# Squares of the group norms on GpSimd, edge copies on ScalarE alone, one modulation group moved from layer 0's gate/up to layer 1's

## The chip, the cores and the metric

The kernel runs on one core of a Trainium2 chip. The metric is the device time of one execution in microseconds (us); three runs of the kernel before gave 2403.01, 2403.49 and 2408.04 us, a median of 2403.49 us. Everything is float32 outside; most matrix products are made from operands split into a high and a low part in the fp32r format.

## The reference

Two layers over 1024 tokens of width 1024. In each layer six vectors (shift, scale and gate for attention and for the feed-forward part) come from a small vector `c`; each of these twelve is called a modulation group here, numbered (layer, group).

```python
for l in range(DEPTH):                                   # DEPTH = 2
    mod = silu(c) @ w_mod[l] + b_mod[l]
    sh_a, sc_a, gt_a, sh_f, sc_f, gt_f = split(mod, 6)   # groups 0..5
    h = rms_norm(x, g_attn[l]) * (1 + sc_a) + sh_a
    # 4 heads A (neighbourhood), 6 heads B (sliding window, sink), 6 heads C (dense)
    ya, yb, yc = attentions(split(h @ w_in[l]))
    y = concat(rms_norm(ya, ga), rms_norm(yb, gb), rms_norm(yc, gc))   # group norms
    x = x + gt_a * (y @ w_o[l])
    h = rms_norm(x, g_ffn[l]) * (1 + sc_f) + sh_f
    gate, up = split(h @ w_gu[l])
    x = x + gt_f * ((silu(gate) * up) @ w_down[l])
return rms_norm(x, g_final)
```

## The kernel before

Each layer runs through the same stages: input projection, attention, output projection, gate/up, down. TensorE (PE) makes all products, VectorE (DVE) and ScalarE (ACT) empty the PSUM banks, split operands and do the softmax, GpSimd (POOL) scales rows and takes some elementwise work, SyncE (SP) issues the DMAs.

**Attention.** One loop over `n` works through 64 pairs of query blocks (24 pairs of C, then 16 of A, then 24 of B; four pairs p = 0 to 3 to a head). A and B heads see a band of keys; their pairs are of class `Band`, and this stretch is called the band. In iteration `n` of the band the engines run in the order in which the code is written (they are pinned): POOL scales the probabilities of pair n+2 (`divide`), DVE makes the low part of pair n-1's turned block (`low`) and adds up the output of pair n-3 (`combine`, tile `y`), PE makes the scores of pair n+4, ACT the exponentials of pair n+3, PE turns pair n's probabilities (`turn`, tiles `T`), and PE multiplies pair n-2 with the values (`pv`). A turned pair has one tile with the four inner blocks and one with the edge blocks (one block of 128x128 for p = 0 and 3, two for p = 1 and 2). ACT casts the inner tile to its high part; the edge tile is copied to the tile `edge`, by DVE for even p and by ACT for odd p. There is one PSUM bank for `pv`, shared by two pairs: after the odd pair, ACT copies half of it (`fold`, tile `cmb`), DVE adds (`combine`), and only then may PE start the next even pair's `pv`.

**Group norms.** When the two heads of a 128-row chunk of `y` are done, `norm_sum` squares the chunk in two halves of 128x512 on ACT, and POOL adds the square to a running sum `gss` (the first chunk of a group is written to `gss` directly). The halves are put into iterations `n + 1` and `n + 2`; the very last chunk's are done on the spot. Some iterations later the sums become factors, and POOL scales the finished chunks with `y<-y,rb`, one 128x512 tile per iteration. ACT also splits finished chunks for the output projection (`y_split`, tile `qk<-y`).

**Modulation groups.** A group needs 1024x1024 weights, times `silu(c)`, summed over rows. DVE does it: 16 steps of 128x512 (`mod_add`, tile `acc`), each after a DMA (`wmt`); then, for each half, DVE splits the sum (`acch`, `accl`), PE sums it over the partitions with two matmuls (`ps_mod`), and DVE picks the diagonal. Groups (0,2) to (0,4) are made during layer 0's attention stage. `mod_stream` spreads further ones over gate/up as a generator:

```python
mods_due = mod_stream(psl, (ntp, "sq", 2, H), (1, 3))   # all groups before (1, 3)
...
    if q >= EARLY:
        next(mods_due, None)
```

So layer 0's gate/up makes (0,5), (1,0), (1,1), (1,2); layer 1's attention stage makes (1,3), (1,4), (1,5); layer 1's gate/up none.

**Gate/up.** 22 column blocks `q` of seven half-size products each (Strassen-like, `PRODUCTS`, index `i`); a product is 12 matmuls of 128x512 into `ps_w`. The first seven `q` take two products each ahead of the loop. DVE and POOL make the sums and low parts of the weights (`ws`, `wpt`), add up products (`u`, `sg`). PE, ACT and DVE are not pinned here; a scheduler has placed their instructions, and each engine runs them in that order. SP's queue is in program order.

All instructions go through one recording helper, so the profile gives nearly all of them line 49; they are told apart by their tiles.

Of the kernel before, what the change touches and what calls it, by code (L numbers as in the profile page):

```python
# [13 lines left out]
AF = mybir.ActivationFunctionType  # L14
ALU = mybir.AluOpType
# [8 lines left out]
H = 512  # L24
# [61 lines left out]
def trunk(ctx: ExitStack, tc, A, C, out):  # L86
    nc = tc.nc
    pe, act, dve, pool, sp = (
        Engine(tc, e) for e in (nc.tensor, nc.scalar, nc.vector, nc.gpsimd, nc.sync)
    )  # L90
# [214 lines left out]
    def mod_add(k, acc, st):  # L305
        ck = condT[:, k : k + 1]
        if k == 0:
            dve.tensor_scalar(out=acc, in0=st, scalar1=ck, scalar2=None, op0=ALU.mult)
        else:
            dve.scalar_tensor_tensor(  # L310
                out=acc, in0=st, scalar=ck, in1=acc, op0=ALU.mult, op1=ALU.add
            )
# [12 lines left out]
    def mod_parts(c, shared):  # L325
        pl, tag, bufs, width = shared
        acc = going["acc"]
        hi = pl.tile([P, width], F32R, name="acch", tag=tag, bufs=bufs)
        lo = pl.tile([P, width], F32R, name="accl", tag=tag, bufs=bufs)
        dve.tensor_copy(hi, acc[:, c])  # L330
        dve.tensor_tensor(out=lo, in0=acc[:, c], in1=f32(hi), op=ALU.subtract)
        going["parts"] = c.start, hi, lo, shared
# [25 lines left out]
    def mod_stream(psp, shared, until):  # L358


        pl, tag, bufs, width = shared
        acc = None
        while todo and todo[0] < until:
            l, g = todo[0]
            first = going["step"]
            if first == 0:
                going["acc"] = cp.tile([P, 1024], F32, name="acc", tag="acc")
            acc = going["acc"]
            halves = [(k, c0) for k in range(first, KC) for c0 in range(0, 1024, width)]
            loads = {}  # L370

            def load(i):
                k, c0 = halves[i]
                st = loads[i] = pl.tile([P, width], F32, name="wmt", tag=tag, bufs=bufs)
                g0 = g * 1024 + c0
                sp.dma_start(st, A["w_mod"][l, k * P : (k + 1) * P, g0 : g0 + width])

            if halves:
                load(0)
                yield  # L380
            for i, (k, c0) in enumerate(halves):
                if i + 1 < len(halves):
                    load(i + 1)
                mod_add(k, acc[:, c0 : c0 + width], loads.pop(i))
                yield
            going["step"] = KC
            mod_parts(slice(0, width), shared)
            while going["step"]:
                yield
                yield  # L390
                mod_flush(psp)
            yield
# [140 lines left out]
    ps_cm, psl = open_pool("ps0", bufs=8, space=PSUM)  # L533
# [285 lines left out]
    for l in range(2):  # L819
# [358 lines left out]
        for oc in range(NE, 8):  # L1178
            w = wab
            for half in range(2):  # L1180
# [3 lines left out]
                if oc == 6 and half == 0:  # L1184
                    close(ps_cm)
                    psS_cm, psS = open_pool("psS", bufs=2, space=PSUM)
                    ps_cm, psl = open_pool("ps2", bufs=4, space=PSUM)
# [8 lines left out]
                i = 2 * (oc - NE) + half  # L1196
# [14 lines left out]
        y = yp.tile([P, 8, S], F32, name="y")  # L1211
# [12 lines left out]
        def gss_tile():  # L1224
            return atp.tile([P, S], F32, name="gss", tag="gss", bufs=1)
# [4 lines left out]
        gss = {23: gss_tile()}  # L1230
        def pt_tile():
            return wp.tile([P, 4, 256], F32R, name="pt", tag="whl", bufs=8)
# [7 lines left out]
        def t_tile():  # L1240
            return psT.tile([P, 4, P], F32, name="T", tag="T")
# [157 lines left out]
        class Band(Pair):  # L1399
# [42 lines left out]
            def turn(self):  # L1442
                pr = self.pr
                T, self.pt = t_tile(), [pt_tile() for _ in range(2)]
                for b in range(2):
                    for i in range(2):
                        pe.transpose(
                            T[:, 2 * b + i, :], pr[:, b, (1 - b + i) * P : (2 - b + i) * P], ident
                        )
                edges = [pr[:, 0, 0:P]] * self.left + [pr[:, 1, 2 * P : 3 * P]] * self.right  # L1450
                E = t_tile()
                for i, src in enumerate(edges):
                    pe.transpose(E[:, i, :], src, ident)
                hi, lo = (
                    t[:, 0:2, :].rearrange("p i (c q) -> p c i q", c=2) for t in self.pt
                )
                T = T.rearrange("p (c i) q -> p c i q", c=2)
                act.copy(hi, T)
                e = self.e = atp.tile([P, 2, P], F32, name="edge", tag="edge", bufs=3)
                (act.copy if self.p % 2 else dve.tensor_copy)(  # L1460
                    e[:, 0 : len(edges)], E[:, 0 : len(edges)]
                )
                self.low = lambda: sub(lo, T, f32(hi))

            def pv(self):
# [38 lines left out]
                return self.z[:, a:b]  # L1504


        def norm_sum(chunks, ss, last, half):

            n = chunks[last]
            c = slice(half * H, (half + 1) * H)  # L1510
            if last == 0:
                act.activation(ss[:, c], y[:, n, c], AF.Square)
                return
            sq = atp.tile([P, H], F32, name="gsq", tag="rb", bufs=2)
            act.activation(sq, y[:, n, c], AF.Square)
            pool.tensor_tensor(out=ss[:, c], in0=ss[:, c], in1=sq, op=ALU.add)

        def norm_scale(chunks, r, psp, tag, engines):
# [76 lines left out]
        N = len(stream)  # L1595
# [5 lines left out]
        for n in range(-AHEAD - 1, N + 3):  # L1601
# [74 lines left out]
            m = n - 1 if n <= NC else n - 3  # L1676
            for end, (chunks, width) in norms.items():
                if begins[end] <= m <= end and (m - begins[end]) % 8 == 7 and (n <= NC or m >= NC):
                    i = (m - begins[end]) // 8
                    if end not in gss:  # L1680
                        gss[end] = gss_tile()
                    for half in range(2):
                        what = lambda a=(chunks, gss[end], i, half): norm_sum(*a)
                        if m == N - 1:
                            what()
                        else:
                            later.setdefault(n + 1 + half, []).append(what)
                    if m == end and end < N - 1:

                        def stats(end=end, width=width, n=n, chunks=chunks):  # L1690
                            r = rstd_cols([gss[end]], width, 8, atp, psT, tag="T", newton=True)

                            def scale():
                                todo = norm_scale(chunks, r, psT, "T", (pool, pool))
                                for i, what in enumerate(todo):
                                    later.setdefault(n + 9 + i, []).append(what)

                            later.setdefault(n + 8, []).append(scale)

                        later.setdefault(n + 5, []).append(stats)  # L1700
# [8 lines left out]
        ps_cm, psl = open_pool("ps1", bufs=4, space=PSUM)  # L1709
# [65 lines left out]
        nt_cm, ntp = open_pool("nt", side="left")  # L1775
# [80 lines left out]
        ps_cm, psl = open_pool("ps3", bufs=8, space=PSUM)  # L1856
# [135 lines left out]
        EARLY = 7  # L1992
# [29 lines left out]
            shifted_sub(b21, b21, shift(2 * i + 1), t2)  # L2022
            h_split("t4", i, b21, dve)

        mods_due = mod_stream(psl, (ntp, "sq", 2, H), (1, 3))
        bs = []
        rows = None
        norm = rstd_rows(ssq, ntp, psl)
# [1 line left out]
        for q in range(EARLY):  # L2030
            for i in range(2):
                a = [w[:, 4 * i : 4 * i + 4] for w in early[q]]
# [20 lines left out]
        for q in range(NF):  # L2053
            if q % 2 == 0:
                gu_start(q // 2)
            if q < EARLY:
                up = q % 2
                e = sg[q // 2][0][:, 0:H]
                if up:
                    (pool if q > 1 else dve).tensor_tensor(  # L2060
                        out=e, in0=e, in1=quads[q]["11"], op=ALU.mult
                    )
            for i, p in enumerate(PRODUCTS[2 if q < EARLY else 0 :]):
                gu_product(q, p, ahead.get())
                if i == 1 and q < EARLY and not up:
                    act.activation(e, quads[q]["11"], AF.Silu)
                ahead.fill()
                g_step()
                if q >= EARLY:
                    next(mods_due, None)  # L2070
        for _ in mods_due:
            pass
# [30 lines left out]
        nt_cm, ntp = open_pool("nt", side="left")  # L2103
# [98 lines left out]
        def square(n, half, tag, bufs):  # L2202
            sq = ntp.tile([P, H], F32, name="sq", tag=tag, bufs=bufs)
            act.activation(sq, xt[:, n, half * H : (half + 1) * H], AF.Square)
            return sq
# [32 lines left out]
        for u in range(NU):  # L2238
            i, t = divmod(u, NB)
# [13 lines left out]
            a, b = ahead.have.pop(0)  # L2253
# [11 lines left out]
            if t < NB - 1:  # L2265
                continue
            m, half = {
                1: (0, 0), 2: (0, 0), 6: (0, 1), 7: (1, 1), 4: (1, 0), 5: (1, 1), 3: (0, 1),
            }[num]
# [132 lines left out]
```

## Time and profile before

| | before |
|---|---|
| runs | 2403.01, 2403.49, 2408.04 us (median 2403.49) |
| profiled execution, its own time | 2405.66 us |
| its span | 2403.9 us, 33342 instructions, mean granted clock 0.993 |
| busy | PE 2337.2, PE weight loads 1954.9, DVE 1756.9, ACT 1192.2, POOL 744.0 us |
| layer 0: C heads, band, gate/up | about 260 to 383, 383 to 491, 590 to 1014 us |
| layer 1: band, gate/up | about 1556 to 1664, 1760 to 2180 us |

A row of the timeline gives start and duration in us, engine, operation, tile written and tiles read, shape, count, and in brackets the idle time of the engine just before it with what ended that. Rows merged with a count give the time of the whole group. In the tables by window, `(x28)` is the number of instructions that ran in that stretch.

### The profile page before, as it was taken

Reading aid. Unit: us, or ns where it says so; the run is one execution under the profiler, and the core shown is the slowest. Engines: PE = TensorE matmul, PEld = TensorE weight load, DVE = VectorE, ACT = ScalarE, POOL = GpSimd, SP = SyncE. Lnnn points to the kernel's source line nnn. Section 1 sums busy time; section 2 is a strip of 40 time slices with the busy share of each in tenths; the row PEclk is TensorE's granted clock in tenths of the full one; section 3 lists DMA queues with packets and bytes.
Section 4 is the critical chain, followed back from the end, with each engine's and each line's share of the span. In section 5 each row is a group of like instructions: output and inputs, shape, how many; then the busy total and the mean of one; then the engine's idle time right before and its main releaser. Section 6 shows DMA issues by size and latency. Waiting matters only on the chain. (4 is left out here: it accounts for less than half of the span.)

```text
span 2403.9 us, 33342 instructions
## 1 busy us (share of the span) xinstructions
PE 2337.2 (97%) x11733; PEld 1954.9 (81%) x11733; DVE 1756.9 (73%) x2788; ACT 1192.2 (50%) x2250; POOL 744.0 (31%) x719
## 2 busy tenths in 40 slices
PE   8999999999999999999999999999999999999998
PEld 4788899888787887888887879988888888888886
DVE  5767898977858788587677679988797554547765
ACT  3422788944543333344543148897454334334443
POOL 1431345610244443300036114465004443430001
PEclk9999999999999999999999999999999999999999
DMA  8458316154345454586424761152534333329633
GB/s 265 138 183 278 94 62 156 45 201 129 109 137 171 155 186 152 174 265 197 155 88 123 246 215 28 44 145 74 199 103 145 114 101 106 122 88 298 213 125 110
DMA packets 305336, 356.95 MB, mean 148 GB/s; under 512 B 51964, under 2 KB 221788, under 8 KB 305168
## 3 DMA queue, kind: packets, MB, share of 16 engines
q1 hardware_dynamic: 283296, 342.07, 44.9%
q10 hardware_dynamic: 21504, 12.59, 2.0%
q8 instruction: 92, 1.51, 0.3%
q14 instruction: 76, 0.62, 0.1%
q0 software_dynamic: 368, 0.17, 0.0%
HBM read 269.79 MB, written 88.63 MB: 149 GB/s over the span
## 5 line engine op out<-in xcount | busy, mean ns | idle before, releaser
L49 PE MATMUL ps_d<-wpt 128*128 128x512 f32 x1848 | 423.8, 390 | 1.1 <-ACT wpt L49 0.7
L49 PEld LDWEIGHTS ps_d<-wpt 128*128 128x128 f32 x1848 | 345.7, 188 | 74.4 <-issue 3.0
L49 POOL TENSOR_SCALAR pr<-pr,rs 128x1024 f32<-128x1024 f32 (+2 forms) x248 | 193.0, 791 | 220.8 <-DVE rs L49 196.8
L49 POOL TENSOR_TENSOR sg<-sg,u 128x512 f32<-128x512 f32 x82 | 116.6, 1422 | 354.0 <-ACT sg L49 228.4
L49 PE MATMUL pv<-pt,vs 128*128 128x256 f32 x1088 | 175.8, 296 | 17.7 <-DVE y L49 13.4
L49 DVE TENSOR_TENSOR pt<-T,pt 128x512 fp32r<-128x512 f32 x272 | 176.9, 678 | 8.3 <-ACT pt L49 8.0
L49 ACT CAST wpt<-w 128x512 fp32r<-128x512 f32 x154 | 95.7, 621 | 174.6 <-PE ps_d L49 156.1
L49 ACT CAST pt<-T 128x512 fp32r<-128x512 f32 x272 | 151.8, 584 | 40.6 <-PE T L49 38.8
L49 ACT COPY u<-ps_w 128x512 f32<-128x512 f32 x128 | 75.1, 587 | 190.1 <-PE ps_w L49 190.1
L49 POOL TENSOR_TENSOR wpt<-ws,wpt 128x512 fp32r<-128x512 f32 x80 | 110.9, 1388 | 186.5 <-ACT wpt L49 140.3
L49 DVE TENSOR_TENSOR wpt<-w,wpt 128x512 fp32r<-128x512 f32 x154 | 108.9, 707 | 79.8 <-ACT wpt L49 77.7
L49 PEld LDWEIGHTS pv<-pt,vs 128*128 128x128 f32 x1088 | 141.7, 190 | 30.8 <-DVE y L49 26.0
L49 PE MATMUL T<-identr,pr 128*128 128x128 f32 x1176 | 161.6, 273 | 0.8 <-DVE edge L49 0.4
L49 PEld LDWEIGHTS T<-identr,pr 128*128 128x128 f32 x1176 | 137.9, 140 | 16.0 <-issue 1.3
L49 DVE SCALAR_TENSOR_TENSOR acc<-wmt,condT,acc 128x512 f32<-128x512 f32 (+1 forms) x98 | 113.9, 1172 | 44.6 <-DMA wmt<-in_w_mod_dram 44.2
L49 ACT CAST wpt<-ws 128x512 fp32r<-128x512 f32 x176 | 107.8, 622 | 60.0 <-issue 28.1
L49 DVE TENSOR_TENSOR wpt<-ws,wpt 128x512 fp32r<-128x512 f32 x96 | 82.9, 872 | 62.0 <-ACT wpt L49 61.9
L49 DVE TENSOR_TENSOR wpt<-graw,wpt 128x512 fp32r<-128x512 f32 x154 | 110.1, 715 | 17.4 <-ACT wpt L49 17.4
L49 ACT CAST wpt<-graw 128x512 fp32r<-128x512 f32 x154 | 95.0, 617 | 52.9 <-DMA graw<-gpd 48.8
L49 DVE TENSOR_REDUCE rs<-sC 128x1 f32<-128x1024 f32 x88 | 107.3, 1221 | 17.7 <-PE sC L49 12.3
L49 DVE TENSOR_TENSOR ws<-wr 128x512 f32<-128x512 f32 x88 | 78.9, 899 | 53.9 <-POOL wpt L49 50.8
L49 PE MATMUL sC<-qk 128*128 128x512 f32 x384 | 107.5, 403 | 5.8 <-ACT pr L49 5.6
(300 smaller groups left out, 5938.0 us busy)
## 6 DMA issues: line engine op xcount, KB each, us to landing
wr<-in_w_gu_dram SPq DMA_DIRECT2D x92, 512.0 KB, 4.1
gpd<-sg SPq DMA_DIRECT2D x154, 256.0 KB, 4.4
graw<-gpd SPq DMA_DIRECT2D x76, 512.0 KB, 3.5
w<-in_w_down_dram SPq DMA_DIRECT2D x110, 256.0 KB, 5.6
wmt<-in_w_mod_dram SPq DMA_DIRECT2D x48, 512.0 KB, 5.3
qk<-qkd SPq DMA_DIRECT2D x44, 512.0 KB, 7.1
wst<-in_w_o_dram SPq DMA_DIRECT2D x32, 512.0 KB, 4.1
wmt<-in_w_mod_dram SPq DMA_DIRECT2D x64, 256.0 KB, 3.6
```

Of the source, the lines that this page charges most:

```text
L49: ins = op(*args, **kwargs)
```

## The change

Three edits. In `Band.turn`, all edge copies go to ACT; those of even p (20 pairs a layer) were on DVE. In `norm_sum`, the square of a chunk is made by POOL as a product of the chunk with itself, except for the last chunk of the layer; that is 14 of 16 squares a layer. In gate/up, layer 0's stream ends before (1,2) and layer 1's stream makes what is left; since the attention stage of layer 1 still makes three groups, these are now (1,2), (1,3), (1,4), and (1,5) falls into layer 1's gate/up. The stream is asked for a step only after five of the seven products of a `q` (not for i = 2 and 5).

```diff
-                (act.copy if self.p % 2 else dve.tensor_copy)(
-                    e[:, 0 : len(edges)], E[:, 0 : len(edges)]
-                )
+                act.copy(e[:, 0 : len(edges)], E[:, 0 : len(edges)])
...
-        def norm_sum(chunks, ss, last, half):
+        def norm_sum(chunks, ss, last, half, late):
...
+            def square(out):
+                if late:
+                    act.activation(out, y[:, n, c], AF.Square)
+                else:
+                    pool.tensor_tensor(out=out, in0=y[:, n, c], in1=y[:, n, c], op=ALU.mult)
+
             if last == 0:
-                act.activation(ss[:, c], y[:, n, c], AF.Square)
+                square(ss[:, c])
                 return
             sq = atp.tile([P, H], F32, name="gsq", tag="rb", bufs=2)
-            act.activation(sq, y[:, n, c], AF.Square)
+            square(sq)
             pool.tensor_tensor(out=ss[:, c], in0=ss[:, c], in1=sq, op=ALU.add)
...
-                        what = lambda a=(chunks, gss[end], i, half): norm_sum(*a)
+                        what = lambda a=(chunks, gss[end], i, half, m == N - 1): norm_sum(*a)
...
-        mods_due = mod_stream(psl, (ntp, "sq", 2, H), (1, 3))
+        mods_due = mod_stream(psl, (ntp, "sq", 2, H), (1 + l, 2 - 2 * l))
...
-                if q >= EARLY:
+                if q >= EARLY and i % 3 != 2:
                     next(mods_due, None)
```

ACT in layer 0's band, among the B heads: `pr` with 385 columns is an exponential, `pt<-T` the cast of the inner blocks, `edge` the copy of the edge blocks, `gsq` a square, `cmb` the copy that frees the `pv` bank. Before, from one `cmb` to the next:

```order
L49 ACTIVATE pr,rs<-pr,rs 128x385 x2
L49 CAST pt<-T 128x2x2x128
L49 ACTIVATE pr,rs<-pr,rs 128x385 x2
L49 CAST pt<-T 128x2x2x128
L49 COPY edge<-T 128x128
L49 ACTIVATE gsq<-y 128x512
L49 COPY cmb<-pv 64x512
```

The same place now:

```order
L49 ACTIVATE pr,rs<-pr,rs 128x385 x2
L49 CAST pt<-T 128x2x2x128
L49 COPY edge<-T 128x256
L49 ACTIVATE pr,rs<-pr,rs 128x385 x2
L49 CAST pt<-T 128x2x2x128
L49 COPY edge<-T 128x128
L49 COPY cmb<-pv 64x512
```

The square is gone from the place just ahead of `cmb`, and the edge copy of the even pair stands between the two pairs of exponentials.

POOL in layer 0's band, at the change from A to B heads, where it also scales the finished C chunks (`y<-y,rb`); `pr<-pr,rs` is the scaling of probabilities. Before:

```order
L49 TENSOR_SCALAR pr<-pr,rs 128x384 x2
L49 COPY pr<-sinkc 128x2
L49 TENSOR_TENSOR y<-y,rb 128x512
L49 TENSOR_SCALAR pr<-pr,rs 128x384 x2
L49 COPY pr<-sinkc 128x2
L49 TENSOR_TENSOR y<-y,rb 128x512
L49 TENSOR_SCALAR pr<-pr,rs 128x384
L49 TENSOR_SCALAR pr<-pr,rs 128x256
```

The same place now:

```order
L49 TENSOR_SCALAR pr<-pr,rs 128x384 x2
L49 COPY pr<-sinkc 128x2
L49 TENSOR_TENSOR y<-y,rb 128x512
L49 TENSOR_TENSOR gss<-y 128x512
L49 TENSOR_SCALAR pr<-pr,rs 128x384 x2
L49 COPY pr<-sinkc 128x2
L49 TENSOR_TENSOR y<-y,rb 128x512
L49 TENSOR_TENSOR gss<-y 128x512
L49 TENSOR_SCALAR pr<-pr,rs 128x384
L49 TENSOR_SCALAR pr<-pr,rs 128x256
```

Two squares stand in two iterations that also hold a scaling of `y`; the scalings of probabilities behind them come later in POOL's row.

DVE in layer 1's gate/up, at the end of a column block `q`. Before:

```order
L49 TENSOR_TENSOR ws<-wr 128x512
L49 TENSOR_TENSOR ws<-wr,ws 128x512
L49 TENSOR_TENSOR sg<-sg,ps_w 128x512
L49 TENSOR_TENSOR wpt<-wr,wpt 128x512 x2
L49 TENSOR_TENSOR u<-u,ps_w 128x512
```

The same place now, where the moved group (1,5) ends:

```order
L49 TENSOR_TENSOR ws<-wr 128x512
L49 TENSOR_TENSOR ws<-wr,ws 128x512
L49 TENSOR_TENSOR sg<-sg,ps_w 128x512
L49 TENSOR_TENSOR wpt<-wr,wpt 128x512
L49 CAST acch<-acc 128x512
L49 TENSOR_TENSOR acc<-ps_mod,identr 128x512
L49 TENSOR_TENSOR accl<-acc,acch 128x512
L49 TENSOR_REDUCE sums<-acc 128x4
L49 TENSOR_TENSOR wpt<-wr,wpt 128x512
L49 TENSOR_TENSOR u<-u,ps_w 128x512
```

Four instructions of the group come between two low parts of weights.

## The prediction

> **What bounds the kernel now.** I read the page's busy line first, then the waits of PE, the table by window, and the timelines of all engines where PE waits.
>
> ```profile
> PE 2337.2 (97%) x11733; PEld 1954.9 (81%) x11733; DVE 1756.9 (73%) x2788; ACT 1192.2 (50%) x2250; POOL 744.0 (31%) x719
> PE pv L49 <- DVE y L49: 13.4, 22, 1.0
> L49 PEld LDWEIGHTS pv<-pt,vs 128*128 128x128 f32 x1088 | 141.7, 190 | 30.8 <-DVE y L49 26.0
> ```
>
> PE is the bound; no edit takes work from it, so only its waits and its clock can change. The largest wait on one tile is that of `pv` for `y`: 13.4 us by the ends of the matmuls, 26.0 us by the start of the weight loads, which is nearer to what PE loses, since modelled ends overlap the wait. That is the band. The other place that the change touches is layer 0's gate/up:
>
> ```profile
> 760.00:770.00 10.00, 10.00 (x46) 8.25 (x45) 9.20 (x10) 3.94 (x7) 5.71 (x5) 1.00 0.57 186
> 770.00:780.00 10.00, 7.36 (x28) 5.53 (x27) 9.87 (x12) 1.73 (x3) 4.55 (x4) 0.91 0.23 66
> 780.00:790.00 10.00, 10.00 (x42) 8.13 (x42) 8.13 (x13) 3.47 (x6) 1.74 (x1) 0.92 0.60 202
> 900.00:910.00 10.00, 8.81 (x38) 6.73 (x37) 9.93 (x18) 3.40 (x7) 2.50 (x3) 1.00 0.18 59
> 950.00:960.00 10.00, 8.61 (x39) 6.79 (x37) 8.38 (x13) 3.07 (x7) 1.85 (x2) 1.00 0.27 88
> 2040.00:2100.00 60.00, 60.00 (x266) 49.70 (x265) 29.82 (x35) 22.55 (x41) 27.18 (x20) 1.00 0.34 111
> ```
>
> The columns are PE, weight loads, DVE, ACT, POOL, the granted clock, and DMA. The last row is undisturbed: 266 matmuls in 60 us, 0.2256 us each, so a full 10 us holds 44.3, and about one more that straddles an edge, 45.3. The two windows from 770 hold 70 instead of 90.6: 20.6 x 0.2256 = 4.6 us lost. The one at 900 lost 7.3 x 0.2256 = 1.6 us, the one at 950 6.3 x 0.2256 = 1.4 us. Together 7.7 us. In the first and third DVE is at 9.87 and 9.93 of 10: it is late. The timeline shows for what:
>
> ```profile
> 765.09 1.78 DVE L49 TENSOR_TENSOR accl<-acc,acch 128x512 fp32r<-128x512 f32 x1
> 769.20 1.67 DVE L49 TENSOR_TENSOR ws<-ws,wr 128x512 f32<-128x512 f32 x1
> 772.67 0.69 DVE L49 TENSOR_TENSOR ws<-wr 128x512 f32<-128x512 f32 x1
> 776.25 0.50 PE L49 MATMUL ps_mod<-acch,onesr 128*128 128x512 f32 x1 [1.16 <-DVE acch L49]
> 778.23 0.79 PE L49 MATMUL ps_mod<-accl,onesr 128*128 128x512 f32 x1 [1.48 <-DVE accl L49]
> 778.82 1.05 PE L49 MATMUL ps_w<-h21h,wpt 128*128 128x512 f32 x2
> 779.67 0.63 PE L49 MATMUL ps_w<-h21l,wpt 128*128 128x512 f32 x1
> ```
>
> PE comes to a modulation group's two sums and DVE has not yet split `acc`. Afterwards two matmuls take from 778.82 to 779.67, 0.43 us each, half speed. So a stall of 1.16 + 1.48 = 2.64 us cost 4.6 us.
>
> **The change part by part: gate/up.** A group is 16 steps on DVE, each behind a DMA:
>
> ```profile
> L49 DVE SCALAR_TENSOR_TENSOR acc<-wmt,condT,acc x56: 735/752/1841, 723.4 to 954.0; 128x512 f32<-128x512 f32 x56
>   DMA wmt<-in_w_mod_dram: 41.5, 25
> ```
>
> In the 250 us of the stream DVE stood still 41.5 us for these DMAs, with its queue behind it; adding that to DVE's busy 8 to 9 of 10 leaves it no reserve. The change takes one of four groups away and asks for steps after five products of seven. A step now has one or two products (2.7 or 5.4 us at 12 x 0.2256) between it and the next, so about half of the DMA waits go, and DVE's load by the stream falls by two sevenths while it runs. The order puts the second pair of sums of a group two products behind the first in (0,5), three in (1,0) and (1,1); before it was two in all. I therefore take the 7.7 us to go but for a late split of about the size of the one at 900, 1.6 us, with a weight of three quarters: 7.7 - 1.2 = 6.5 us gained. Bounds: 7.7 us if none is left; if one 4.6 us stall stays, 3.1 us.
>
> PE's four sums per group move to layer 1, 4 x 0.2256 = 0.9 us out and in: nothing. SP's `wmt` loads move too; ahead of them in its queue nothing waits longer than before. In layer 1 the new steps meet a DVE at 29.82 of 60 (the row at 2040), and at the place where the group's splits now stand DVE was idle:
>
> ```profile
> 1961.18 0.69 DVE L49 TENSOR_TENSOR ws<-wr 128x512 f32<-128x512 f32 x1 [3.25 <-POOL wpt L49]
> 1967.18 0.69 DVE L49 TENSOR_TENSOR wpt<-wr,wpt 128x512 fp32r<-128x512 f32 x1 [3.51 <-ACT wpt L49]
> ```
>
> The 3.51 us gap is where the order shows `acch`, `acc`, `accl`, `sums`, four instructions of about 0.7 us. I charge 0.4 us, a quarter of the 900 stall; bounds 0 and the 1.6 us itself. Gate/up: -6.5 + 0.4 = -6.1 us, from -7.7 to -1.5.
>
> The Trainium skill bears on the half speed ("TensorE: Matmul & The Clock Gate", Part 1): the array drops to half clock after an idle window of about 3.4 us. The gaps here were shorter, 1.16 and 1.48 us, and the clock dropped nevertheless; by the rule taken strictly only the 2.64 us could come back from that place, and the total would be 2.0 us less.
>
> **The band: the squares and the edge copies.** The path at each change of the `pv` bank is: end of the odd `pv`, `cmb` on ACT, `y` on DVE, next `pv`. First a head with a square, then one without:
>
> ```profile
> 433.30 0.63 ACT L49 ACTIVATE gsq<-y 128x512 f32<-128x512 f32 x1
> 433.96 0.58 ACT L49 COPY cmb<-pv 64x512 f32<-64x512 f32 x1
> 434.57 0.68 DVE L49 TENSOR_TENSOR y<-pv,cmb 64x512 f32<-64x512 f32 x1 [0.30 <-ACT cmb L49]
> 435.31 0.74 PE L49 MATMUL pv<-pt,vs 128*128 128x256 f32 x4 [0.63 <-DVE y L49]
> 465.61 0.27 ACT L49 COPY edge<-T 128x128 f32<-128x128 f32 x1
> 466.09 0.58 ACT L49 COPY cmb<-pv 64x512 f32<-64x512 f32 x1 [0.21 <-PE pv L49]
> 467.45 0.74 PE L49 MATMUL pv<-pt,vs 128*128 128x256 f32 x4 [0.31 <-DVE y L49]
> 389.60 0.37 ACT L49 COPY edge<-T 128x256 f32<-128x256 f32 x1
> 389.86 0.64 ACT L49 ACTIVATE gsq<-y 128x512 f32<-128x512 f32 x1
> 390.39 0.61 ACT L49 ACTIVATE pr<-pr,rs 128x384 f32<-128x384 f32 x1
> ```
>
> With the square in front, PE waits 0.63 us; without, 0.31. So a square ahead of `cmb` costs 0.32 us; there are two such places a layer, four in all. On ACT a square holds the queue 390.39 - 389.86 = 0.53 us, a two-block edge copy 389.86 - 389.60 = 0.26. The new edge copy of p = 2 goes ahead of `cmb` by two exponentials and a cast; ACT has 0.21 us of idle time there (the row at 466.09), which hides all but about 0.07 us (0.02 more for spacing between ACT's instructions). The new one of p = 0 falls into the other half of the head, where the square of every second head stood and did no harm; it costs nothing while that 0.53 us slot is empty.
>
> Sum over both layers: four heads gain 0.32 - 0.07 = 0.25, that is 1.0 us. In three more places a layer ACT has no gaps (the start of the band, the stretch that scales the A chunks, the first splits of `w_o`), and there its net change counts, 0.53 - 0.26 = 0.27 us, six times 1.6 us. Some six plain heads a layer lose 0.07: 0.8 us. DVE loses its copies,
>
> ```profile
> 431.59 0.42 DVE L49 COPY edge<-T 128x256 f32<-128x256 f32 x1
> ```
>
> 20 a layer, but at 434.57 it waits for ACT, so this pays only where `y` is late by DVE itself, once a layer behind the statistics: I take half a copy, 0.2 us, twice. The band: -1.0 - 1.6 + 0.8 - 0.2 = -2.0 us. Bounds: if all 0.07s become the full 0.26 and no loaded place gains, 12 x 0.26 - 1.0 = +2.1 us; if DVE's copies pay fully in the loaded places, -4 us. In the C heads ACT loses six squares a layer and PE has no wait there: 0.
>
> **POOL's side.** The squares add 28 x 1.3 us to POOL. Its scalings of probabilities come ahead of PE's turning by a margin; the tightest I found, with pairs counted back from the last, is this one:
>
> ```profile
> 418.51 1.04 POOL L49 TENSOR_SCALAR pr<-pr,rs 128x384 f32<-128x384 f32 x2
> 419.64 1.29 POOL L49 TENSOR_TENSOR y<-y,rb 128x512 f32<-128x512 f32 x1
> 420.92 1.04 POOL L49 TENSOR_SCALAR pr<-pr,rs 128x256 f32<-128x256 f32 x2
> 424.82 0.71 PE L49 MATMUL T<-identr,pr 128*128 128x128 f32 x5
> 453.46 1.60 POOL L49 TENSOR_SCALAR pr<-pr,rs 128x384 f32<-128x384 f32 x2 [2.02 <-ACT pr L49]
> 434.02 1.27 POOL L49 TENSOR_TENSOR gss<-gss,gsq 128x512 f32<-128x512 f32 x1 [0.55 <-ACT gsq L49]
> ```
>
> The scaling that starts at 420.92 ends at 421.96, and its turning starts at 424.82: 2.86 us of margin. The order puts two squares ahead of it, 2 x 1.29 = 2.58. So 0.28 us are left, and I charge nothing; beyond that PE waits.
>
> Total: -6.1 - 2.0 = -8.1 us. The profiled execution took 2405.66 us (span 2403.9), which is 2.2 above the median; 2405.66 - 8.1 = 2397.6, and against the median 2403.49 - 8.1 = 2395.4 us.
>
> **The rivals.** *The stalls come back elsewhere* (chance 0.22). DVE is in order, and the 1.67 and 1.78 us rows above show that an instruction can take 2.5 times its 0.69; a few of these ahead of a split stall PE again. For it: the first group keeps two products between its sums. Against: the idle gaps of 3.25 and 3.51 us. If one 4.6 us stall stays in layer 0 and a 1.6 us one arises in layer 1, gate/up gains 1.5 us, and with the band at -1.0 the time is 2401.0 us.
>
> *POOL becomes the bound of the band* (0.12), the slower side. The two squares eat the margin to 0.28 us. If scalings take 1.60 us as at 453.46, not 1.04, six in a row add 3.4 us, and PE waits about 3 us. There are two crowds a layer (the scaling of the C chunks and of the A chunks), four in all: 12 us, less the 6.1 us from gate/up: 2403.49 + 5.9 = 2409.4 us. It decides from 0.05 us per scaling on. Against it: at 434.02 POOL adds while DVE's `y` at 434.57 takes its usual 0.68, and the scalings beside it are at 1.04.
>
> The Trainium skill has a rule behind it ("SBUF — State Buffer", Who interferes with whom): DVE instructions with both inputs in SBUF and GpSimd instructions exclude one another. The trace agrees: `ws` at 769.20 took 1.67 us and the 434.57 row, which reads PSUM, did not lengthen. By that rule the squares meet only the `y_split` and `w_o` low parts here.
>
> That the edits do not take effect is no rival: the order shows each.
>
> **How the numbers follow.** The forecast has 0.66, its own range 2403.49 - 11.7 = 2391.8 to 2403.49 - 4.8 = 2398.7 us. The range given takes in the first rival too, up to the bound of -1.5 for gate/up with +1.5 in the band: 2391.5 to 2403.5, which leaves out the second. A difference of 0.2% (4.8 us) is about the least that a measurement can tell from none. Faster: the forecast and a little of the first rival, 0.68; same: the rest of it, 0.2; slower: 0.12.
>
> **What would show it.** Right: in layer 0's gate/up no window under 44 matmuls but one, and the clock at 1.00 there; the wait of `pv` for `y` 0.31 to 0.40 in every plain head, none at 0.63; no wait of `T` for POOL's `pr`. Wrong: a `ps_mod` stall with half-speed matmuls in layer 1 (first rival), or `T` waiting for `pr` at the change from A to B heads (second). If `pv` waits 0.5 us or more in plain heads, ACT had less room than the 0.21 us row says.

## The result and the profile after

The changed kernel takes 2395.14 us (median of 16 runs, 2393.01 to 2401.63); the kernel before, run beside it, 2402.89 us (2398.92 to 2412.84). The ratio is 0.9966, interval 0.9959 to 0.9972: 7.75 us faster by the medians. The profiled execution of after took 2398.09 us with a span of 2396.3, 7.6 us less than before.

The busy line and the largest wait of the page, then the group of `pv` weight loads, of after:

```profile
PE 2338.5 (98%) x11733; PEld 1958.2 (82%) x11733; DVE 1747.8 (73%) x2748; ACT 1186.4 (50%) x2262; POOL 776.9 (32%) x747
PE pv L49 <- DVE y L49: 11.8, 21, 1.3
L49 PEld LDWEIGHTS pv<-pt,vs 128*128 128x128 f32 x1088 | 142.2, 191 | 28.6 <-DVE y L49 23.8 <-ACT pt L49 3.6
```

POOL is busy 33 us more, DVE 9 less. `pv` waits for `y` 1.6 us less by matmuls (13.4 to 11.8) and 2.2 less by weight loads (26.0 to 23.8). No wait of PE for `acch` or `accl` is left in either layer's gate/up. The table by window of after (PE, weight loads, DVE, ACT, POOL, clock, DMA), layer 0's gate/up:

```profile
770.00:780.00 10.00, 10.00 (x46) 8.26 (x44) 9.80 (x11) 3.28 (x6) 6.20 (x5) 1.00 0.63 195
780.00:790.00 10.00, 9.84 (x43) 7.80 (x42) 9.81 (x14) 3.89 (x8) 2.91 (x2) 1.00 0.38 134
900.00:910.00 10.00, 10.00 (x46) 8.29 (x45) 5.85 (x10) 4.46 (x8) 4.94 (x3) 1.00 0.37 122
950.00:960.00 10.00, 10.00 (x45) 8.23 (x45) 5.18 (x9) 4.33 (x8) 2.58 (x2) 1.00 0.54 186
980.00:990.00 10.00, 9.27 (x41) 7.62 (x41) 2.46 (x4) 5.86 (x11) 3.85 (x3) 1.00 0.08 17
```

The four windows that held 28, 42, 38 and 39 matmuls hold 46, 43, 46 and 45. A small new hole stands at 980: PE waits 0.73 us there for ACT's `sg`. Why the stalls are gone shows in the timeline of after at the first group's sums:

```profile
794.79 0.39 PE L49 MATMUL ps_mod<-accl,onesr 128*128 128x512 f32 x1
795.45 0.42 DVE L49 CAST acch<-acc 128x512 fp32r<-128x512 f32 x1
795.78 0.68 DVE L49 TENSOR_TENSOR acc<-ps_mod,identr 128x512 f32<-128x512 f32 x1
796.39 0.68 DVE L49 TENSOR_TENSOR accl<-acc,acch 128x512 fp32r<-128x512 f32 x1
800.51 0.39 PE L49 MATMUL ps_mod<-acch,onesr 128*128 128x512 f32 x1
```

DVE splits the second half 1.6 us behind the first sums and is done at 797.07, 3.4 us before PE asks. In the kernel before it had a queue there and PE stood 2.64 us. The band of after, at the head that had a square ahead of `cmb`:

```profile
434.59 1.03 POOL L49 TENSOR_TENSOR gsq<-y 128x512 f32<-128x512 f32 x1
434.90 0.27 ACT L49 COPY edge<-T 128x128 f32<-128x128 f32 x1
435.20 0.58 ACT L49 COPY cmb<-pv 64x512 f32<-64x512 f32 x1
435.81 0.68 DVE L49 TENSOR_TENSOR y<-pv,cmb 64x512 f32<-64x512 f32 x1
436.55 0.74 PE L49 MATMUL pv<-pt,vs 128*128 128x256 f32 x4 [0.36 <-DVE y L49]
```

The wait is 0.36 us, it was 0.63.

One stretch got slower, the start of layer 0's gate/up. Before, then after, from the timelines:

```profile
578.45 1.05 ACT L49 CAST whi<-wst 128x1024 fp32r<-128x1024 f32 x1 [3.15 <-DMA wst<-in_w_gu_dram]
583.01 1.05 PE L49 MATMUL ps_st<-onesr,ssq 128*128 128x1 f32 x8 [0.57 <-DVE ssq L49]
```

```profile
580.16 1.05 ACT L49 CAST whi<-wst 128x1024 fp32r<-128x1024 f32 x1 [4.34 <-DMA wst<-in_w_gu_dram]
584.72 1.05 PE L49 MATMUL ps_st<-onesr,ssq 128*128 128x1 f32 x8 [1.68 <-DVE ssq L49]
587.53 0.63 PE L49 MATMUL ps_w<-h11h,wlo 128*128 128x512 f32 x1
587.95 0.63 PE L49 MATMUL ps_w<-h11l,whi 128*128 128x512 f32 x1
```

The stage's first product starts at 576.83 before and 577.45 after. Counted from there, a weight load of the stage lands 1.1 us later in after. The squares of `xb` on ACT stand behind its cast, so PE waits 1.1 us more (1.68 instead of 0.57) and then runs six matmuls at half speed (0.42 us from start to start, 0.23 elsewhere). The stretch is 2.7 us longer. Of the nine traces here with most squares on POOL five have the half speed (the stretch is 1.9 to 2.9 us longer) and four do not (0.2 to 0.4); none of the five with the squares on ACT has it. With one trace of each kernel this makes it likely, but does not show, that the squares bring it on. The length of the wait does not decide it: the half speed followed waits of 0.93 to 1.89 us at this place and did not follow others of up to 1.15 us.

### The profile page after: what moved, and what is told of

It reads as the page before. It is cut to its first block, busy times and chain, and to the rows that moved or that the text cites. A ratio compares the mean times of both kernels' runs of the same rounds, so it can differ in the third digit from the quotient of the medians.

```text
span 2396.3 us, 33342 instructions
## 1 busy us (share of the span) xinstructions
PE 2338.5 (98%) x11733; PEld 1958.2 (82%) x11733; DVE 1747.8 (73%) x2748; ACT 1186.4 (50%) x2262; POOL 776.9 (32%) x747
## 5 line engine op out<-in xcount | busy, mean ns | idle before, releaser
L49 PE MATMUL ps_d<-wpt 128*128 128x512 f32 x1848 | 423.8, 390 | 1.0 <-ACT wpt L49 0.7
L49 PE MATMUL pv<-pt,vs 128*128 128x256 f32 x1088 | 176.3, 297 | 16.1 <-DVE y L49 11.8
L49 PEld LDWEIGHTS pv<-pt,vs 128*128 128x128 f32 x1088 | 142.2, 191 | 28.6 <-DVE y L49 23.8
```

The lines of the kernel that those rows point to most:

```text
L49: ins = op(*args, **kwargs)
```

## The experiments

Three stages of each trace, both layers for the band with the output projection (from the 381st `pv` of a layer to its first `ps_w`), each worked out from one trace by the start times in the timeline and compared with the same stage of before (380.4, 436.7 and 423.8 us). The last column is what the runs say of the whole time. In gate/up 0 five rows contain the slow start with half speed (1.9 to 2.9 us): the change, the squares alone, edges and squares, the last three chunks and the mix. The rest of a span (C heads, down projection) differs between executions by up to 6 us.

| kernel | band | gate/up 0 | gate/up 1 | time ratio to before (interval) |
|---|---|---|---|---|
| the change | -3.2 | -5.5 | +0.3 | 0.9966 (0.9959 to 0.9972) |
| modulation edit alone | -0.3 | -7.7 | +1.3 | 0.9977 (0.9969 to 0.9986) |
| edge copies alone | +1.1 | -0.1 | -0.2 | 1.0008 (0.9999 to 1.0016) |
| squares alone | +4.5 | +3.6 | +0.2 | 1.0017 (1.0008 to 1.0025) |
| edges and squares | -2.9 | +1.4 | 0.0 | 0.9992 (0.9983 to 1.0000) |
| change without pacing | -3.2 | -4.1 | +4.1 | 1.0003 (0.9993 to 1.0013) |
| pacing alone | +0.1 | +8.1 | +0.2 | 1.0034 (1.0021 to 1.0046) |
| squares made twice | +14.3 | -6.9 | +1.7 | 1.0037 (1.0024 to 1.0051) |
| squares of the last three chunks on ACT | -2.0 | -5.5 | +1.1 | 0.9966 (0.9953 to 0.9978) |
| squares of the last two chunks on ACT | -3.3 | -7.5 | +1.9 | 0.9970 (0.9958 to 0.9981) |
| mixed by stretch | -0.6 | -5.4 | +2.6 | 0.9979 (0.9970 to 0.9988) |
| before, a product more between splits and sums | -0.2 | +2.7 | -0.4 | 1.0021 (1.0012 to 1.0030) |
| change without pacing, a product more there | -3.0 | +0.5 | +1.5 | 0.9992 (0.9983 to 1.0000) |

**The modulation edit alone**

```diff
-        mods_due = mod_stream(psl, (ntp, "sq", 2, H), (1, 3))
+        mods_due = mod_stream(psl, (ntp, "sq", 2, H), (1 + l, 2 - 2 * l))
-                if q >= EARLY:
+                if q >= EARLY and i % 3 != 2:
```

> Only the modulation edit. Theory A, the parts of the forecast add up: -6.1 us against the kernel before (the trace of the changed kernel would make it -6 to -9, less what a later start of the clock takes back). The band is as before, so pv waits for y 0.63 in the heads with a square; no wait of ps_mod for acch or accl in either layer. Rival B, the stalls were the price of DVE's load and only change place: -1.5 us or less, with a ps_mod wait of 1 us or more somewhere.

Measured 2399.25 against 2404.57 us: -5.3, by the ratio -5.5 (-7.5 to -3.4). Theory A. No `ps_mod` wait is left in either layer's gate/up.

**The edge copies alone**

```diff
-                (act.copy if self.p % 2 else dve.tensor_copy)(
-                    e[:, 0 : len(edges)], E[:, 0 : len(edges)]
-                )
+                act.copy(e[:, 0 : len(edges)], E[:, 0 : len(edges)])
```

> Only the edge copies, the squares still on ACT. Theory A, ACT is what is short in the band: the copy pays its full 0.26 us behind the four squares and in the six loaded places (10 x 0.26 = 2.6 us), 0.07 in some twelve plain heads (0.8 us), DVE gives back 0.4: +3.0 us. Rival B, DVE is what is short in the band: its 40 copies of 0.42 us come off the path in one place of ten or more: -1 to -2 us.

Measured 2405.82 us, +1.2, by the ratio +1.9 (-0.2 to +3.8). The sign is theory A's, though the interval takes in zero; the band lost 1.1 us in the trace, less than the 3.0. Its timeline, where a square and the new copy meet ahead of `cmb`:

```profile
417.55 0.64 ACT L49 ACTIVATE gss<-y 128x512 f32<-128x512 f32 x1
419.64 0.39 ACT L49 COPY edge<-T 128x256 f32<-128x256 f32 x1
420.05 0.58 ACT L49 COPY cmb<-pv 64x512 f32<-64x512 f32 x1
421.40 0.74 PE L49 MATMUL pv<-pt,vs 128*128 128x256 f32 x4 [0.76 <-DVE y L49]
```

ACT comes late by the two together. A cycle of the band is the time from one `pv` that waits for `y` to the next; this one takes 5.37 us instead of 4.69.

**The squares alone**

```diff
-                act.activation(ss[:, c], y[:, n, c], AF.Square)
+                square(ss[:, c])
...
-            act.activation(sq, y[:, n, c], AF.Square)
+            square(sq)
```

with `square` as in the change.

> Only the squares on POOL, the edge copies as before. Theory A, ACT is what is short: four heads gain 0.32 us each and six loaded places 0.53 us each, 1.3 + 3.2: -4.5 us, more than with the edge copies beside it. Rival B, POOL's squares lengthen DVE's instructions with two inputs in SBUF, and DVE then has its own copies too: -1 us or less, and y late in the heads where POOL works.

Measured 2408.31 us, +3.7, by the ratio +4.1 (+1.9 to +6.0): slower, and this is where the forecast's reasons fail. The two heads with a square ahead of `cmb` do gain 0.30 and 0.32 us each, as expected (4.77 to 4.47 and 4.78 to 4.46). Six other cycles of layer 0, most of them in the loaded places, lose 0.2 to 0.9 us where theory A had three gain 0.53. They lose it in three ways. The first is at the end of the band, shown before and then with the squares alone:

```profile
481.64 1.21 DVE L49 TENSOR_TENSOR wlo<-wst,whi 128x1024 fp32r<-128x1024 f32 x1
482.78 0.68 DVE L49 TENSOR_TENSOR pt<-T,pt 128x512 fp32r<-128x512 f32 x1
483.38 0.67 DVE L49 TENSOR_TENSOR y<-pv,cmb 64x512 f32<-64x512 f32 x1
```

```profile
480.95 1.47 POOL L49 TENSOR_TENSOR gsq<-y 128x512 f32<-128x512 f32 x1
482.49 1.62 POOL L49 TENSOR_TENSOR gss<-gss,gsq 128x512 f32<-128x512 f32 x1
482.89 2.31 DVE L49 TENSOR_TENSOR wlo<-wst,whi 128x1024 fp32r<-128x1024 f32 x1
485.12 0.68 DVE L49 TENSOR_TENSOR pt<-T,pt 128x512 fp32r<-128x512 f32 x1
485.72 0.67 DVE L49 TENSOR_TENSOR y<-pv,cmb 64x512 f32<-64x512 f32 x1
```

Beside POOL's addition the `w_o` low part, both inputs in SBUF, takes 2.31 us instead of 1.21, and `y` stands behind it in DVE's queue: this cycle loses 0.89 us by rival B's mechanism. The second and third way are in other cycles of the kernel with the squares alone:

```profile
456.61 0.72 ACT L49 ACTIVATE qk<-y,vecs 128x512 fp32r<-128x512 f32 x1 [0.96 <-POOL y L49]
424.16 0.49 DVE L49 CUSTOM_DVE_ANT_0 pr<-sB,bz,sinkc 128x256 f32<-128x256 f32 x1 [0.25 <-POOL pr L49]
```

Behind the statistics (where the sums have become factors) ACT's split `qk<-y` waits 0.96 us for POOL's scaled `y`, and `cmb` stands behind it; this cycle loses 0.93 us. These splits for the output projection are not pinned, and the scheduler has put them elsewhere in ACT's row: the split that waits stands ahead of this `cmb` here, and the first split that needs POOL's scaled `y` stood behind it before. In a plain head, one without a square ahead of `cmb`, DVE waits for the sink column that POOL copies, `y` follows late, and the cycle loses 0.53 us. The last two are neither theory's mechanism.

**Edges and squares together, without the modulation edit**

> Edge copies and squares, without the modulation edit. Theory A: -2.0 us (between -1.5 and -2.5), and the waits of the band as in the changed kernel; together with the kernel that has the modulation edit alone it gives the whole change. Rival B: it is worth no more than the edge copies alone. Rival C, POOL becomes the bound of the band: slower than before, and T waits for pr.

Measured 2402.72 us, -1.9 (by the ratio -4.1 to 0.0). Theory A in the sum. With the modulation edit alone it makes -5.5 - 1.9 = -7.4, the change measured -8.2 by its ratio: the two halves add up within their intervals. Within the band nothing adds: +1.1 and +4.5 alone, -2.9 together.

**The change without the pacing**

```diff
-                if q >= EARLY and i % 3 != 2:
+                if q >= EARLY:
```

> The changed kernel without the pacing: the group moves to layer 1, and steps are asked for after every product again. Theory A, the stalls come from the DMA waits and the dense steps (the reason given in the prediction): they come back in layer 0, and the time is 3 to 6.5 us above the changed kernel's, -1.2 to -4.7 against the kernel before, with a ps_mod wait for acch or accl. Rival B, the number of groups in layer 0 is what matters: within 1.5 us of the changed kernel.

Measured 2404.32 us, +0.3 against before (ratio 1.0003), some 8 above the changed kernel: theory A, and more than it said. The stalls are back, and in layer 1 there is one:

```profile
774.59 0.50 PE L49 MATMUL ps_mod<-acch,onesr 128*128 128x512 f32 x1 [1.47 <-DVE acch L49]
776.27 0.50 PE L49 MATMUL ps_mod<-accl,onesr 128*128 128x512 f32 x1 [1.18 <-DVE accl L49]
1938.40 0.49 PE L49 MATMUL ps_mod<-acch,onesr 128*128 128x512 f32 x1 [1.17 <-DVE acch L49]
1940.38 0.50 PE L49 MATMUL ps_mod<-accl,onesr 128*128 128x512 f32 x1 [1.48 <-DVE accl L49]
```

Its trace (span 2398.0) belongs to one of its shortest runs (2399.54 to 2410.67), so the trace shows the stalls but not their usual price.

**The pacing alone** (on the kernel before, six products of seven so that four groups fit; no group moves)

```diff
-                if q >= EARLY:
+                if q >= EARLY and i != 2:
```

> The kernel before with the pacing alone: no group moves, no step after the third product of a round of seven. Theory A, pacing is what removes the stalls: -3 to -5.5 us against the kernel before. Rival B, the four groups now fill 88 of 90 places, DVE has the same work and the stalls only move: 0 to -1.5 us.

Measured 2412.06 us, +8.1: outside both theories. The `ps_mod` waits shrink to 0.98 us and less, but the fourth group ends with the stage, and there its loads and splits stand in DVE's queue in front of what PE needs:

```profile
983.05 0.92 SPq L49 DMA_DIRECT2D wmt<-in_w_mod_dram  x2
986.53 0.75 DVE L49 SCALAR_TENSOR_TENSOR acc<-wmt,condT,acc 128x512 f32<-128x512 f32 x1 [1.07 <-DMA wmt<-in_w_mod_dram]
988.33 0.68 DVE L49 TENSOR_TENSOR u<-u,ps_w 128x512 f32<-128x512 f32 x1
990.20 1.22 PE L49 MATMUL ps_w<-ht3h,wpt 128*128 128x512 f32 x2 [7.43 <-ACT sg L49]
```

With four groups the stream has no room for the pacing. As it now runs to the end of the stage, this run prices that end as much as the pacing, and no run separates the two.

**The squares made twice on POOL** (the changed kernel, the instruction repeated)

> The changed kernel with each square on POOL made twice. Theory A, the margin of POOL is the 0.28 us that the prediction worked out: the two more squares of 1.29 us ahead of the scaling make T wait for pr some 2.3 us in each of four crowds, +9 us against the changed kernel, +1 against the kernel before, with rows of T waiting for POOL's pr. Rival B, POOL has room by more than the order shows, since the scalings it is late with are asked for early: +2 us or less, no wait of T for pr. Rival C, the second square lengthens DVE's two-input instructions beside it: +2 to +5 us with pv waiting for y and none of T for pr.

Measured 2413.14 us, +9.2 against before and so about 17 above the change. POOL does become the bound of the band when the margin is gone, and harder than expected. At the tightest place:

```profile
420.33 2.15 POOL L49 TENSOR_TENSOR gss<-y 128x512 f32<-128x512 f32 x2
423.10 1.00 PE L49 MATMUL T<-identr,pr 128*128 128x128 f32 x5 [0.44 <-POOL pr L49]
423.67 0.62 DVE L49 CUSTOM_DVE_ANT_0 pr<-sB,bz,sinkc 128x384 f32<-128x384 f32 x1 [2.08 <-POOL pr L49]
428.01 0.74 PE L49 MATMUL pv<-pt,vs 128*128 128x256 f32 x4 [1.50 <-DVE y L49]
```

`T` waits 0.44 us for the scalings, but DVE 2.08: its next row sums need the sink column that POOL copies behind the squares (`pr<-sinkc`), and `y` stands behind them.

**The squares of the last three chunks on ACT again** (the changed kernel; these chunks are of the B heads, where the expectations here and below say A)

```diff
-  what = lambda a=(chunks, gss[end], i, half, m == N - 1): norm_sum(*a)
+  what = lambda a=(chunks, gss[end], i, half, m >= 47): norm_sum(*a)
```

> The changed kernel with the squares of the last three A chunks on ACT again, those of all other chunks on POOL. Theory A, in the loaded places DVE sets y and POOL's squares lengthen its low halves: the end of the band goes back to the 17.6 us of the kernel with the edge copies alone (18.1 in the changed one), 0.5 us a layer: -1.0 us against the changed kernel (-2 to 0). Rival B, the forecast's reason, ACT's net work counts in these places: four squares a layer cost 0.53 us each, +2 to +4 us.

Measured 2396.28 us, ratio 0.9966: no difference from the change. Both are half right: the last three cycles of the band go from 18.1 to 17.6 us, and the stretch behind the statistics gives 0.9 back (two of its cycles go from 4.50 to 4.77 and from 4.91 to 5.29 us).

**The last two chunks only** (`m >= 55`)

> The changed kernel with the squares of the last two A chunks only on ACT. Theory A, DVE sets y at the end of the band and POOL's squares there lengthen its low halves: the last three cycles of the band go from 18.07 us to 17.5 and nothing else moves, 0.5 us a layer: -1.0 us against the changed kernel. Rival B, ACT's two squares push cmb: the cycles before the end lose as much, 0 to +1 us.

Measured 2397.51 us, ratio 0.9970: no difference that can be told. The last three cycles take 17.7 instead of 18.1, theory A's direction at half its size.

**Mixed by stretch** (`m >= 47`, and every second edge copy of B heads 2 to 4 on DVE)

> The changed kernel, but behind the statistics (three B heads) every second edge copy on DVE as before, and the squares of the last three A chunks on ACT. Theory A, each stretch of the band has its own late engine, ACT behind the statistics and DVE at the start and the end: five cycles go from 26.8 to 25.7 us, the last three from 18.07 to 17.6, 1.6 us a layer: -3.2 us against the changed kernel. Rival B, the stretches hang together, what a head gains the next one waits for: 0 to -1 us.

Measured 2400.00 us, ratio 0.9979: some 3 us above the changed kernel, outside both. One cycle behind the statistics went from 6.37 to 7.20 us. The stretches do hang together, as rival B says, and no version of the band clearly beat the change.

**A product more between splits and sums** (the kernel before)

```diff
             while going["step"]:
                 yield
                 yield
+                yield
                 mod_flush(psp)
```

> The kernel before with one product more between a group's splits and the sums that read them, and nothing else: all four groups stay, a step after every product. Theory A, a stall is only the distance of the second sums from the first (DVE's queue is late there by the 2.65 us that PE waits, and one product is 2.7 us): no ps_mod wait over 0.4 us is left and the time is 4 to 6.5 us below the kernel before. Rival B, DVE's load by the stream is what makes it late, and a product more only moves the stalls: within 1.5 us of the kernel before.

Measured 2408.31 us, +4.8 (by the ratio +2.9 to +7.2): outside both. No `ps_mod` wait is left, as theory A has it, but the time goes the other way, as the waits of PE in layer 0's gate/up show:

```profile
PE ps_w L49 <- ACT sg L49: 4.7, 2, 2.9
PE ps_w L49 <- ACT u L49: 2.9, 2, 1.9
```

The stalls have moved to the copies that empty the product banks: rival B's mechanism, at a higher price than it said.

**The same on the change without its pacing**

> The kernel with the band's edits and the moved group but no pacing, with one product more between splits and sums. Theory A, the pacing does nothing but make this distance: the time is the changed kernel's, -7 to -9 us against the kernel before, without a ps_mod wait over 0.4 us. Rival B, the pacing works through the load: as the kernel with the move alone, 0 to -2 us.

Measured 2402.15 us, -1.3, by the ratio -1.9 (-4.1 to 0.0): rival B. Distance between splits and sums is not what the pacing gives; PE waits for `sg` 3.0 and `u` 2.9 us in layer 0's gate/up instead.

## Why the prediction came out right

**The sum.** Predicted 2395.4, measured 2395.14; -6.1 for the modulation edit (alone -5.5, -7.5 to -3.4) and -2.0 for the band (-1.9, -4.1 to 0.0). Its own terms give 0.2 us more: it takes 0.2 us for DVE's copies "twice", which is 0.4, and adds 0.2.

**Gate/up: the place was right, one reason was not.** All three stalls went. No split was late, for which 1.2 us were kept; the hole at 980, four matmuls or 0.9 us, is a wait for `sg`. Layer 1 cost 0.3 us in this trace against the 0.4 charged, but 1.1 to 2.6 us in the five other traces with the same edit there, so that the term was small. And "about half of the DMA waits go" is wrong. DVE's waits for the modulation loads in layer 0, and the steps of the stream, of after:

```profile
DVE acc L49 <- DMA wmt<-in_w_mod_dram: 47.5, 24, 5.3
L49 DVE SCALAR_TENSOR_TENSOR acc<-wmt,condT,acc x42: 737/752/1789, 726.0 to 957.6; 128x512 f32<-128x512 f32 x42
```

They were 41.5 us for four groups (64 steps; the row counts all but the first two of a group) and are 47.5 for three (48): each step waits longer. What the runs show in its place is that moving and pacing work only together: moving alone takes the band's -1.9 us to +0.3, pacing alone (six places of seven) gives +8.1, both together -5.3 us. Taking the wait at the sums away by distance turns it into a wait at the banks. So DVE must be free when either consumer asks: by the waits, three groups spread over 75 places leave it so, four groups over 90 or three packed densely do not.

**The first rival** (stalls come back elsewhere) did not happen in the change, but it is what the move alone, the pacing alone and the product more did. Of the signs of being right, two were missed. The part of layer 0's gate/up with the stream has two windows under 44 matmuls (43 at 780, 41 at 980), where one was allowed. One plain head waits 0.45 us, above the 0.40 named.

**The half speed.** It was charged at 4.6 us for 2.64 of stall. In the trace without pacing the same stall (1.17 + 1.48) was followed by matmuls at full pace, three in 0.69 us, and cost 3.2:

```profile
1940.72 0.63 PE L49 MATMUL ps_w<-h21h,wpt 128*128 128x512 f32 x2
1941.19 0.39 PE L49 MATMUL ps_w<-h21l,wpt 128*128 128x512 f32 x1
1941.41 0.62 PE L49 MATMUL ps_w<-h21h,wpt 128*128 128x512 f32 x2
```

So the drop is not tied to the stall alone; what else decides it no run here shows. The Trainium skill ("TensorE: Matmul & The Clock Gate", Part 1) ties it to an idle window of about 3.4 us. Here it followed single waits of 0.93 to 1.89 us at the start of gate/up and did not follow two of 2.65 us in all.

**The band: the sum was right, the engine was wrong.** The heads with a square gained 0.26 us each (4.77 to 4.51, 4.78 to 4.52), as predicted 0.25. The six plain heads were charged 0.42 us a layer; they lost 0.14 and 0.03 where `cmb` waits for ACT and 0.22 in one other, 0.39. The three loaded places were charged -0.8 us a layer and gave 0.5 at the start, nothing behind the statistics, 0.5 at the end: -0.9.

The step that failed is the reason for these: "ACT has no gaps ..., and there its net change counts", with DVE's copies put at 0.2 us. By that, the squares alone would gain 4.5 us and the copies alone would cost; the squares alone lost 4.1. At the start one cycle goes from 4.79 to 4.44 us with the copies alone and does not change with the squares alone. The last three cycles, 18.54 us before, take 17.55 with the copies alone and 19.31 with the squares alone. DVE's row sets `y` in these two places. Behind the statistics it is POOL's results that come late: the squares alone lose 1.6 us a layer there, the copies alone 0.3, both together 0.1. The DVE term was mis-sized: with the squares on POOL the edge copies are worth 2.9 + 4.5 = 7.4 us of the band, without them they cost 1.1. How much of the 7.4 is DVE's time is not shown, because with the copies in ACT's row the scheduler also places the splits differently, and in after none of them waits for POOL.

The cycles make about -2.1 us for both layers, as forecast, but the table has -3.2. With the copies on ACT 33 matmuls of the output projection stand in the last three cycles, where there were 31; these two, 0.45 us a layer, account for most of the rest. The forecast has no term for them.

**POOL.** The margin was given as 2.86 - 2.58 = 0.28 us. A square with one input twice takes 1.04 us (1.48 in 4 of 28), not the 1.29 of an addition, so two of them are 2.08 and 0.78 is left; in after the scaling ends at 425.25 and its turning starts at 426.19. No turning waits. The consumer was named wrongly: the first to wait is DVE, for POOL's sink column, in after 0.36 us at one place:

```profile
425.41 0.48 DVE L49 CUSTOM_DVE_ANT_0 pr<-sB,bz,sinkc 128x256 f32<-128x256 f32 x1 [0.36 <-POOL pr L49]
```

That is the plain head that lost 0.14 us. With the squares doubled POOL is the bound, as the second rival has it, but mostly by way of DVE.

**Errors that cancel.** That the total came out within 0.3 us is in part luck. In the trace the band gained 1.2 us more than forecast. Layer 0's gate/up gained 5.5 us where 6.5 were forecast; without the 2.7 us of its slow start it would be 8.2, and traces without that start have 6.9 to 7.7. The slow start, which the forecast did not have, and a layer 1 dearer than charged lie on the other side of these gains.

## What to carry to other kernels

Where an engine works in order and two others wait for it at different points, moving one consumer away only changes the place of the wait; the load has to go down and be spread at once, so test such an edit as a pair. Before an operation is moved from ACT to POOL, ask which engine sets the path in each stretch: two-input work on POOL lengthened DVE's two-input work beside it, POOL's other results came later, and the move paid only together with something taken from DVE. Look at the order too: a scheduler that places part of an engine's row moves other work when one instruction leaves. An engine's margin is the least over all its consumers, small copies included, not that of the largest one.

## What the runs showed of the hardware that was not expected

A DVE subtraction of 128x1024 with both inputs in SBUF took 2.31 us beside POOL's square and addition and 1.21 in the kernel before. There POOL was the one that waited: its two scalings beside the subtraction took 2.96 us, where two took 1.04 at 418.51. The Trainium skill ("SBUF — State Buffer", Who interferes with whom) has DVE instructions with two inputs in SBUF contend with GpSimd instructions that read SBUF. The rows agree.

POOL's product of a tile with itself took 1.04 us, a sum of two tiles 1.28.

The same 2.65 us stall of PE cost 4.75 us in the kernel before and 3.2 in another, by whether the half speed followed. At the start of layer 0's gate/up the half speed followed waits of 0.93 to 1.89 us in five traces and did not follow 0.34 to 1.15 us in nine. A 256 KB weight load there landed 1.1 us later in after, and the stretch cost 2.7 us more with the half speed behind it; why the load was late is open.
